# Advancing an attention pipeline by query block, both heads at once, instead of head by head

## The chip, the cores and the metric

The kernel runs on one core of one Trainium2 chip. The metric is device time in microseconds (us) of one execution. A core has five engines with queues of their own: TensorE (PE; its weight loads are listed as PEld), VectorE (DVE), ScalarE (ACT), GpSimd (POOL) and SyncE (SP), which issues the DMAs here. TensorE writes its results to PSUM, an accumulator memory; the other tiles lie in SBUF.

## What is computed

Two layers, each with one combined input projection, four groups of four attention heads (64 wide, sequence 1024, query blocks of 128 rows), a gate, an output projection and a layer norm:

```python
def hybrid_layer(x, ...):
    p = split_columns(einsum("bsd,de->bse", x, w_in))
    ...
    for i in range(S // Q_BLOCK):            # 8 query blocks of 128
        o_a = stick_breaking_block(a_q[:, q0:q1], a_k[:, :q1], a_v[:, :q1], qpos, kpos)
        o_b = diff_block(b_q[:, q0:q1], b_k[:, :q1], b_v[:, :q1], causal, bias_b, lam, lam_init, subln)
        o_c = dsa_block(...)                 # an indexer's top 256 keys, then softmax
        o_d = mla_block(...)
    y = concatenate(outs) * silu(p["gate"])
    y = einsum("bse,ed->bsd", y, w_out)
    return layer_norm(ALPHA * x + y, ln_g, ln_b)

def stick_breaking_block(q, k, v, qpos, kpos):
    z = einsum("bqhd,bkhd->bhqk", q, k) * HEAD_DIM ** -0.5
    log1m = where(strict, log_sigmoid(-z), 0.0)
    after = cumsum(log1m, axis=3, reverse=True) - log1m
    w = where(strict, exp(log_sigmoid(z) + after), 0.0)
    return einsum("bhqk,bkhd->bqhd", w, v)

def diff_block(...):                         # two softmax maps per head
    a = p[:, 0] - lam * p[:, 1]
    o = einsum("bhqk,bkhd->bqhd", a, v)
    return rms_norm(o, subln) * (1.0 - lam_init)
```

## The kernel before

The four groups are called a (stick-breaking), b (differential), c (sparse) and d (latent). Each has two units of two heads: a0, a1, d0, d1, b0, b1, c0, c1, in this order in a layer (`ORDER`, L42), after two units s0 and s1 that make the indexer's scores. Units walk over the eight query blocks; block i has n = 128 (i + 1) keys. A generator runs a unit and yields after each piece; between pieces the main loop (L1115) runs a stretch of background work (`Background`, `BGSEQ`): the input projections of later units, the gates, and from b1 on the output projection of the groups that are done (`g_out`). How much is a quota in us from `ORDER`, shared over a unit's steps by the weight (i + W0), W0 = 2. `with_topk` lays pieces of the top-k search (VectorE) between the steps of a0 and a1.

A unit (`softmax_pair`) has three stages per block. Stage 1 makes the scores of both heads in PSUM (`stick` for a, `on_rows` for the others) and turns them into weights in SBUF. In `stick` each head has a score buffer of its own, and per head five ScalarE instructions (absolute value, relu, exponential, logarithm, and the last exponential), a scan that runs backwards and a subtraction on VectorE. In `on_rows` VectorE scales and takes the minimum, ScalarE exponentiates; unit b has two maps per head, and from block 4 on two chunks of 512 keys. Stage 2 transposes a head's weights in blocks of 128 x 128 on TensorE into PSUM, from where ScalarE copies them to the tile PT (`transposed`); for b it first combines the two maps. Stage 3 multiplies PT and the values into one PSUM tile of four blocks (pv); after four blocks it multiplies the softmax sums out (rl) and `finalize` applies the gate and stores to y_d. For b `finalize` also makes the RMS norm: a square, a product with a matrix of 1/256 on TensorE (ms_b), a logarithm and an exponential.

`push` (L363) holds a queue of stages and advances by head: stage 1 of block i (with head 0), a stretch of projections, head 1's transposes of block i - 1; then for head 1 a second stretch, the values of block i - 1, head 0's transposes of block i.

PSUM has four tags: sc (two buffers of 1024 columns, the scores), mm (two of 512, the projections' sums, and in b and c the second transpose tile), tr (one of 512: transposes, rl, ms_b and others) and pv (one of 512). SBUF tiles of tag p (eight) hold weights, PT and results of the background; tag h (four halves) holds gates, outputs and the output projection's operands. The framework waits for data and buffers by itself, and its planner lays down the order on each engine before the program runs: code order is priority, and what it takes to be ready goes first. `Paced` passes matmuls through, so that their line is L92 or L95; no instruction is pinned by it here (`PIN_S` is 0).

Of the kernel before, what the change touches and what calls it, by code (L numbers as in the profile page):

```python
# [21 lines left out]
P = 128  # L22
# [21 lines left out]
TR_MM, PT_DVE = ('b0', 'b1', 'c0', 'c1'), ()  # L44
OUT_DVE = 1
PIN_A, PIN_S = 2, 0
OUT_AT = ('b1', 0.3)
FRAC, W0, W1 = 1, 2, 0.5
# [29 lines left out]


class Paced:  # L80


    def __init__(self, tc):
        self.tc, self.pin = tc, False

    def _issue(self, ins):
        if self.pin:
            self.tc.keep_in_program_order(ins)
        self.pin = False

    def matmul(self, *a, **k):
        self._issue(self.tc.nc.tensor.matmul(*a, **k))  # L92

    def transpose(self, *a, **k):
        self._issue(self.tc.nc.tensor.transpose(*a, **k))  # L95
# [3 lines left out]
def trunk(ctx: ExitStack, tc: tile.TileContext, t: dict, out: bass.AP, depth=DEPTH, dbg=None):  # L99
# [223 lines left out]
    def finalize(g, et, c, pv, gs, rl, subv):  # L323
        if g != 1:
# [3 lines left out]
        else:  # L328
            o = half("o_h")
            nc.scalar.activation(o, pv, AF.Copy)  # L330
            nc.vector.tensor_tensor(o, rl, o, op=ALU.mult)
            sq = half("sq_h")
            nc.scalar.activation(sq, o, AF.Square)
# [8 lines left out]
        nc.sync.dma_start(y_d[YPOS[et]][:, 512 * c:512 * c + 512], gs)  # L342

    def transposed(p, i, g, pair):
        nblk = i + 1
        pt = wrk([P, nblk, P], F32, "PT")
        for j0 in range(0, nblk, 4):
            m = min(4, nblk - j0)
            tr = mm_ps("trp") if j0 and f"{'abcd'[g]}{pair}" in TR_MM else tr_ps("trp")
            for j in range(m):  # L350
                te.transpose(tr[:, P * j:P * j + P], p[:, P * (j0 + j):P * (j0 + j) + P], ident)
            if j0 and f"{'abcd'[g]}{pair}" in PT_DVE:
                nc.vector.tensor_copy(pt[:, j0:j0 + m, :], tr[:, :P * m].rearrange("p (j n) -> p j n", j=m))
            else:
                with ahead(HP_T):
                    nc.scalar.activation(pt[:, j0:j0 + m, :], tr[:, :P * m].rearrange("p (j n) -> p j n", j=m), AF.Copy)  # L356
        return pt

    queue = []
    back = None  # L360
    te = Paced(tc)

    def push(w, pin, *stages):  # L363

        te.pin = pin & 1
        stages[0]()
        yield FRAC * w
        for it in list(queue):
            te.pin = pin & 2 if len(it) > 1 else pin & 4
            it.pop(0)()  # L370
            if not it:
                queue.remove(it)
        te.pin = False
        if len(stages) > 1:
            queue.append(list(stages[1:]))
        yield (1 - FRAC) * w

    def flush():
        while queue:
            for it in list(queue):  # L380
                it.pop(0)()
                if not it:
                    queue.remove(it)

    def softmax_pair(g, pair, scores, nmaps, nbt, scale, v, neglam=None, subv=None):
# [6 lines left out]
        def stick(i):  # L392

            n = P * (i + 1)
            z = {(h, 0): sc_ps("z") for h in range(2)}
# [3 lines left out]
            for h in range(2):  # L399
                zh = z[h, 0][:, :n]  # L400
                e, r = wrk([P, n], F32, "spe"), wrk([P, n], F32, "P0")

                nc.scalar.activation(e, zh, AF.Abs)
                nc.scalar.activation(r, zh, AF.Relu)
                nc.scalar.activation(e, e, AF.Exp, scale=-1.0)
                nc.scalar.activation(e, e, AF.Ln, bias=1.0)  # L406
                nc.vector.tensor_tensor_scan(backwards(r, n), backwards(r, n), backwards(e, n), 0.0, ALU.add, ALU.add)  # L407
                nc.vector.tensor_tensor(r, zh, r, op=ALU.subtract)
                nc.scalar.activation(r, r, AF.Exp)
                st[i]["res", h] = [r]  # L410

        def on_rows(i):

# [3 lines left out]
            p = {hm: wrk([P, n], F32, f"P{hm[1]}") for hm in maps}  # L417
            mx = {hm: small([P, 3], F32, "mx") for hm in maps}
            low = {hm: 3e38 for hm in maps}
            far = env["ns"].get(i) if g == 2 else None  # L420
            used = 0
            for o in range(0, n, 512):
# [5 lines left out]
                for lo, hi in ((o, min(o + w, near)), (a, o + w)):  # L428
                    if lo >= hi:
                        continue  # L430
                    for h, m in maps:
                        out = mx[h, m][:, used:used + 1]
# [7 lines left out]
                    used += 1  # L440
            for h, m in maps:
                nc.scalar.activation(p[h, m], p[h, m], AF.Exp, bias=low[h, m], scale=-1.0,  # L442
                                     accum_out=st[i]["ls"][:, m, h, i % 4:i % 4 + 1])
            for h in range(2):
                st[i]["res", h] = [p[h, m] for m in range(nmaps)]

        def stage1(i, h):
            i4 = i % 4
            if i4 == 0 and h == 0:
                st["ls"] = small([P, nmaps, 2, 4], F32, "ls", tag="ls", bufs=2)  # L450
            if h == 0:
                st[i] = dict(ls=st["ls"], pts=[])
            if h == 0:
                (on_rows if g else stick)(i)

        def stage2(i, h):
# [14 lines left out]
            d["pts"].append(transposed(p, i, g, pair))  # L471

        def stage3(i, h):
            if h == 0:
                return
# [6 lines left out]
            for j in range(i + 1):  # L482
                for hh in range(2):
                    te.matmul(pv[64 * hh:64 * hh + 64, P * i4:P * i4 + P], v[j // 4][:, j % 4, vo + 64 * hh:vo + 64 * hh + 64],
# [4 lines left out]
            elif i4 == 3:  # L489

                rl = tr_ps("rl")
                for k in range(4):
                    for hh in range(2):
                        te.matmul(rl[64 * hh:64 * hh + 64, P * k:P * k + P],
# [3 lines left out]
        for i in range(NB):  # L498
            for h in range(2):
                yield from push((i + W0) / (16 * W0 + 56), PIN_S, lambda: stage1(i, h), lambda i=i, h=h: stage2(i, h),  # L500
                                lambda i=i, h=h: stage3(i, h))
# [9 lines left out]
    for l in range(depth):  # L511
# [504 lines left out]
        def products(ps, maps, ops, i, o, w, rows_of, first=True, last=True):  # L1016

            qh, ql, kh, kl = ops
            for k, (x, y) in enumerate(((qh, kh), (ql, kh), (qh, kl))):
                for hm in maps:  # L1020
                    r = rows_of(*hm)
                    te.matmul(ps[hm][:, :w], x[r, P * i:P * i + P], y[r, o:o + w], start=first and k == 0,
                              stop=last and k == 2, tile_position=(r.start, 0))

        def score_a(pair):
            def f(ps, maps, i, o, w, near):
                tail = o + w == P * (i + 1)
                products(ps, maps, env[f"a{pair}t"], i, o, w, lambda h, m: slice(64 * h, 64 * h + 64), last=not tail)
                if tail:
                    for hm in maps:  # L1030
                        te.matmul(ps[hm][:, w - P:w], u_b, id_b, start=False, stop=True)
# [7 lines left out]
        def score_c(pair):  # L1039
            def f(ps, maps, i, o, w, near):  # L1040
# [3 lines left out]
                if msk:  # L1044
                    for hm in maps:
                        te.matmul(ps[hm][:, a - o:w], id_b, ns[i][:, a:o + w], start=False, stop=True)
            return f

        def score_d(pair):
            def f(ps, maps, i, o, w, near):  # L1050
# [3 lines left out]
                for k, (y, n) in enumerate(((krh, 64), (krl, 32))):  # L1054
                    for h, m in maps:
                        te.matmul(ps[h, m][:, :w], rq[64 * h:64 * h + n, P * i:P * i + P], y[64 * h:64 * h + n, o:o + w],
                                  start=False, stop=k == 1 and not tail, tile_position=(64 * h, 0))
                if tail:
                    for hm in maps:
                        te.matmul(ps[hm][:, w - P:w], id_b, v_b, start=False, stop=True)  # L1060
# [239 lines left out]
```

## Time and profile before

| | |
|---|---|
| median of 3 runs | 1829.26 us (1827.39 to 1833.37) |
| the profiled execution | 1826.64 us, span 1824.8 us |
| TensorE busy | 1680.8 us (92%), 10886 matmuls |
| VectorE busy | 1155.1 us (63%) |
| ScalarE busy | 860.9 us (47%) |
| GpSimd busy | 445.8 us (24%) |
[...]
| DMA | 205.70 MB, mean 113 GB/s |

Busy time counts an instruction from its start to its end; matmuls overlap, so the distance from one start to the next tells their cost better than their length. A timeline merges neighbouring instructions of a kind (x4); its first number is the first one's start. In brackets behind a row stands the engine's idle time before it, and what ended that.

### The profile page before, as it was taken

What the parts mean: (1) busy time and instruction counts of PE and PEld (TensorE: products, weight loads), DVE (VectorE), ACT (ScalarE), POOL (GpSimd) and SP (SyncE); (2) the same over time, 40 slices, a digit from 0 to 9 for tenths busy, and PEclk for the clock granted to TensorE, in tenths of its full rate; (3) what the DMA queues carried; (4) which work ended last, traced back from release to release, by engine and by line L of the source; (5) the groups of instructions that cost most, each with busy time, mean ns of one, the idle gap of its engine ahead of it and who ended that gap; (6) DMA issues with size and microseconds to landing.
All of it is one profiled execution on the core that took longest, in us unless ns stands there. A gap on an engine that the chain in (4) does not pass through costs nothing. (4 is left out here: it accounts for less than half of the span.)

```text
span 1824.8 us, 29123 instructions
## 1 busy us (share of the span) xinstructions
PE 1680.8 (92%) x10886; PEld 1246.0 (68%) x10886; DVE 1155.1 (63%) x2605; ACT 860.9 (47%) x1715; POOL 445.8 (24%) x406
## 2 busy tenths in 40 slices
PE   7998888899999999899999997989999999988997
PEld 5686666677676776576777765757776767765775
DVE  5777788865346445454866778898553555554448
ACT  3436757533355443345434466574334454433452
POOL 4232123422122312110322321233212222212012
PEclk9999979999999999899999998999999999998999
DMA  6221122525223236544331211235242322565343
GB/s 190 76 90 39 35 96 76 186 84 162 105 77 109 81 118 217 165 152 138 141 90 39 95 35 48 83 118 191 64 145 93 110 93 76 165 197 163 111 145 110
DMA packets 117034, 205.70 MB, mean 113 GB/s; under 512 B 11113, under 2 KB 41369, under 8 KB 116889
## 3 DMA queue, kind: packets, MB, share of 16 engines
q1 hardware_dynamic: 116888, 203.81, 33.9%
q8 instruction: 86, 1.41, 0.3%
q14 instruction: 60, 0.48, 0.1%
HBM read 131.92 MB, written 71.32 MB: 111 GB/s over the span
## 5 line engine op out<-in xcount | busy, mean ns | idle before, releaser
L236 PE MATMUL ps_pj<-xh,whi 128*128 128x512 f32 x832 | 349.2, 420 | 13.0 <-ACT xh L527 9.9
L197 POOL TENSOR_SCALAR whi<-wraw 128x512 fp32r<-128x512 f32 (+1 forms) x154 | 114.8, 746 | 923.1 <-PE ps_pj L236 573.8
L236 PE MATMUL ps_pj<-xl,whi 128*128 128x512 f32 x832 | 335.6, 403 | 0.4 <-DVE xl L528 0.4
L236 PE MATMUL ps_pj<-xh,wlo 128*128 128x512 f32 x832 | 334.7, 402 | 0.0
L356 ACT ACTIVATE PT<-trp 128x512 f32<-128x512 f32 (+3 forms) x384 | 182.0, 486 | 314.5 <-PE trp L95 307.6
L442 ACT ACTIVATE P<-P,mx 128x128 f32<-128x128 f32 (+7 forms) x256 | 195.9, 767 | 137.8 <-DVE mx L436 63.1
L95 PE MATMUL trp<-ident,P 128*128 128x128 f32 x1152 | 198.5, 287 | 32.9 <-ACT PT L356 12.0
L198 POOL TENSOR_TENSOR wlo<-wraw,whi 128x512 fp32r<-128x512 f32 (+1 forms) x154 | 216.0, 1403 | 14.0 <-PE ps_pj L236 1.4
L95 PEld LDWEIGHTS trp<-ident,P 128*128 128x128 f32 x1152 | 131.4, 142 | 101.1 <-ACT PT L356 33.4
L236 PEld LDWEIGHTS ps_pj<-xh,whi 128*128 128x128 f32 x832 | 160.2, 192 | 56.8 <-issue 23.1
L92 PE MATMUL pv<-PT,v 128*64 128x128 f32 x2304 | 190.1, 284 | 3.2 <-ACT PT L356 3.0
L236 PEld LDWEIGHTS ps_pj<-xh,wlo 128*128 128x128 f32 x832 | 159.6, 192 | 36.7 <-issue 2.6
L236 PEld LDWEIGHTS ps_pj<-xl,whi 128*128 128x128 f32 x832 | 160.7, 193 | 33.4 <-issue 5.2
L92 PEld LDWEIGHTS pv<-PT,v 128*64 128x64 f32 x2304 | 137.6, 138 | 60.0 <-issue 43.8
L438 DVE TENSOR_SCALAR_CACHE_REDUCE P<-ps_r 128x512 f32<-128x512 f32 (+3 forms) x160 | 83.4, 567 | 139.8 <-PE ps_r L92 120.2
L92 PE MATMUL ps_r<-op 64*128 64x512 f32 (+7 forms) x1152 | 156.5, 389 | 3.7 <-DVE P L438 3.0
L849 DVE SCALAR_TENSOR_TENSOR S<-rel,iw,S 128x512 f32<-128x512 f32 (+3 forms) x140 | 109.9, 787 | 36.4 <-ACT rel L843 30.6
L874 DVE TENSOR_SCALAR_CACHE_REDUCE junk<-S,t 128x1024 bf16<-128x1024 f32 (+1 forms) x132 | 124.2, 941 | 2.9
L407 DVE TENSOR_TENSOR_SCAN P<-P,spe 128x128 f32<-128x128 f32 (+7 forms) x64 | 91.8, 1435 | 43.3 <-ACT spe L406 43.3
L92 PEld LDWEIGHTS ps_r<-op 32*128 32x128 f32 (+1 forms) x1152 | 81.5, 184 | 55.1 <-issue 34.6
L258 PE MATMUL ps_v<-whi,xh 128*128 128x256 f32 x384 | 112.6, 294 | 0.3 <-DVE kl L296 0.3
L258 PE MATMUL ps_v<-wlo,xh 128*128 128x256 f32 x384 | 110.3, 288 | 0.0
(231 smaller groups left out, 2866.3 us busy)
## 6 DMA issues: line engine op xcount, KB each, us to landing
wraw<-in_wqk_dram SPq DMA_DIRECT2D x104, 256.0 KB, 2.6
g_d<-gate SPq DMA_DIRECT2D x32, 256.0 KB, 2.0
gs_h<-g_d SPq DMA_DIRECT2D x32, 256.0 KB, 3.7
y_d<-gs_h SPq DMA_DIRECT2D x32, 256.0 KB, 2.1
yraw<-y_d SPq DMA_DIRECT2D x32, 256.0 KB, 3.4
part_d<-xo SPq DMA_DIRECT2D x32, 256.0 KB, 2.7
tt<-part_d SPq DMA_DIRECT2D x16, 512.0 KB, 6.5
wraw<-in_wv_dram SPq DMA_DIRECT2D x24, 256.0 KB, 3.0
```

Source lines behind the costliest of these rows:

```text
L92: self._issue(self.tc.nc.tensor.matmul(*a, **k))
L95: self._issue(self.tc.nc.tensor.transpose(*a, **k))
L197: nc.gpsimd.tensor_scalar(hi, raw, 1.0, 0.0, op0=ALU.mult, op1=ALU.add)
L198: nc.gpsimd.tensor_tensor(lo, raw, fb(hi), op=ALU.subtract)
L236: nc.tensor.matmul(ps, a[:, k4, :], b[:, kb, 512 * c:512 * c + 512], start=(n == 0), stop=(n == 23))
L258: nc.tensor.matmul(pv, a[:, kb, P * sb:P * sb + P], b[:, k2, :], start=(n == 0), stop=(n == 23))
L356: nc.scalar.activation(pt[:, j0:j0 + m, :], tr[:, :P * m].rearrange("p (j n) -> p j n", j=m), AF.Copy)
L407: nc.vector.tensor_tensor_scan(backwards(r, n), backwards(r, n), backwards(e, n), 0.0, ALU.add, ALU.add)
L438: nc.vector.tensor_scalar(dst, src, -scale, low[h, m], op0=ALU.mult, op1=ALU.min, accum_out=out)
L442: nc.scalar.activation(p[h, m], p[h, m], AF.Exp, bias=low[h, m], scale=-1.0, accum_out=st[i]["ls"][:, m, h, i % 4:i % 4 + 1])
L849: nc.vector.scalar_tensor_tensor(s[:, o:o + w], r[:, h, :w], sc, s[:, o:o + w], op0=ALU.mult, op1=ALU.add)
L874: ins = nc.vector.tensor_scalar(junk[:, :P * (i + 1)], arr[i], th, None, op0=op, op1=ALU.add, accum_out=dst[:, k:k + 1])
```

## The change

`push` becomes `step`, which advances one query block with both heads: the scores of block i and both heads' transposes of block i - 1 (where there are two score chunks, b from block 4 on, the transposes alternate with them), one stretch of projections of twice the length, then the values of block i - 1. The normalisation product of b and what follows it is put off by one block. Transposes alternate between the buffers tr and mm in all units. In `stick` both heads share one score buffer for n up to 512, and ScalarE's five instructions and the subtraction do both at once. `Paced` goes, so that the matmuls of the pipeline carry their own lines.

```diff
-    def push(w, pin, *stages):
-        te.pin = pin & 1
-        stages[0]()
-        yield FRAC * w
-        for it in list(queue):
-            te.pin = pin & 2 if len(it) > 1 else pin & 4
-            it.pop(0)()
-            if not it:
-                queue.remove(it)
-        te.pin = False
-        if len(stages) > 1:
-            queue.append(list(stages[1:]))
-        yield (1 - FRAC) * w
+    pipe = dict(turn=[], values=[], late=[])
+
+    def step(w, scores, turn, values):
+        old = pipe["turn"], pipe["values"]
+        for k in range(max(len(scores), len(old[0]))):
+            for stage in (scores, old[0]):
+                if k < len(stage):
+                    stage[k]()
+        yield w
+        after(old[1])
+        pipe.update(turn=turn, values=values)
+
+    def after(values):
+        late, pipe["late"] = pipe["late"], []
+        for f in late + values:
+            f()
...
-            tr = mm_ps("trp") if j0 and f"{'abcd'[g]}{pair}" in TR_MM else tr_ps("trp")
+            tr = (mm_ps if k + j0 // 4 & 1 else tr_ps)("trp")
...
     def finalize(g, et, c, pv, gs, rl, subv):
...
+        def norm():
             ms = tr_ps("ms_b")
             for h in range(2):
                 r = slice(64 * h, 64 * h + 64)
-                te.matmul(ms[r], on256[r, :64], sq[r], start=True, stop=True)
+                nc.tensor.matmul(ms[r], on256[r, :64], sq[r], start=True, stop=True)
             nc.scalar.activation(sq, ms, AF.Ln, bias=eps_r, scale=4.0)
             nc.scalar.activation(sq, sq, AF.Exp, scale=-0.5)
             nc.vector.scalar_tensor_tensor(o, o, subv[:, 0:1], sq, op0=ALU.mult, op1=ALU.mult)
             nc.vector.tensor_tensor(gs, o, gs, op=ALU.mult)
+            out()
+
+        pipe["late"].append(norm)
...
         def stick(i):
             n = P * (i + 1)
-            z = {(h, 0): sc_ps("z") for h in range(2)}
+            if n <= 512:
+                zs = [sc_ps("z").rearrange("p (h n) -> p h n", h=2)[:, :, :n]]
+                z = {(h, 0): zs[0][:, h] for h in range(2)}
+            else:
+                zs = [sc_ps("z").unsqueeze(1)[:, :, :n] for _ in range(2)]
+                z = {(h, 0): zs[h][:, 0] for h in range(2)}
...
-            for h in range(2):
-                zh = z[h, 0][:, :n]
-                e, r = wrk([P, n], F32, "spe"), wrk([P, n], F32, "P0")
+            for k, zh in enumerate(zs):
+                nh = 2 // len(zs)
+                e, r = wrk([P, nh, n], F32, "spe"), wrk([P, nh, n], F32, "P0")
                 nc.scalar.activation(e, zh, AF.Abs)
                 nc.scalar.activation(r, zh, AF.Relu)
                 nc.scalar.activation(e, e, AF.Exp, scale=-1.0)
                 nc.scalar.activation(e, e, AF.Ln, bias=1.0)
-                nc.vector.tensor_tensor_scan(backwards(r, n), backwards(r, n), backwards(e, n), 0.0, ALU.add, ALU.add)
+                for h in range(nh):
+                    rb, eb = backwards(r[:, h], n), backwards(e[:, h], n)
+                    nc.vector.tensor_tensor_scan(rb, rb, eb, 0.0, ALU.add, ALU.add)
                 nc.vector.tensor_tensor(r, zh, r, op=ALU.subtract)
                 nc.scalar.activation(r, r, AF.Exp)
...
         for i in range(NB):
-            for h in range(2):
-                yield from push((i + W0) / (16 * W0 + 56), PIN_S, lambda: stage1(i, h), lambda i=i, h=h: stage2(i, h),
-                                lambda i=i, h=h: stage3(i, h))
+            yield from step((i + W0) / (8 * W0 + 28), stage1(i), [lambda i=i, h=h: stage2(i, h) for h in range(2)],
+                            [lambda i=i: stage3(i)])
```

`stage1` now returns a list: one function, or in b one for each chunk of 512 keys.

## Rows read from the trace of the kernel before

**Rows 1.** The page, first section: busy us, share of the span, instructions.

```profile
PE 1680.8 (92%) x10886; PEld 1246.0 (68%) x10886; DVE 1155.1 (63%) x2605; ACT 860.9 (47%) x1715; POOL 445.8 (24%) x406
```

**Rows 2.** The view of cores: span and mean granted clock.

```profile
core 0: 1824.8 us, clock 0.966
```

**Rows 3.** TensorE's waits: line, tile, what ended them; us in total, times, longest.

```profile
PE z L92 <- DVE P L408: 21.2, 18, 2.6
PE trp L95 <- ACT PT L356: 12.0, 18, 2.1
...
PE z L92 <- ACT rel L843: 8.0, 4, 3.1
...
PE ms_b L92 <- ACT sq_h L333: 6.4, 8, 1.5
PE ps_r L92 <- DMA krr<-kr_d: 5.7, 2, 3.2
...
PE trp L95 <- ACT sq_h L338: 3.3, 6, 0.8
...
PE trp L95 <- DVE hl L286: 0.4, 2, 0.2
```

**Rows 4.** Windows of a0 with a1, and c1: span, busy by engine, clock, DMA share.

```profile
141.00:368.00 227.00, 196.72 (x1089) 145.21 (x1089) 189.28 (x334) 145.04 (x265) 61.75 (x57) 0.92 0.26 86
...
827.00:866.00 39.00, 38.17 (x333) 26.23 (x330) 17.10 (x72) 23.25 (x54) 2.51 (x2) 1.00 0.38 127
```

**Rows 5.** Timeline of TensorE, a block of d0: start, us, instruction.

```profile
424.75 0.66 PE L95 MATMUL trp<-ident,P 128*128 128x128 f32 x4
425.34 0.73 PE L92 MATMUL ps_r<-op 64*128 64x512 f32 x4
...
431.61 0.39 PE L236 MATMUL ps_pj<-xh,wlo 128*128 128x512 f32 x1
431.84 0.60 PE L95 MATMUL trp<-ident,P 128*128 128x128 f32 x4
432.19 0.48 PE L236 MATMUL ps_pj<-xh,whi 128*128 128x512 f32 x1
```

**Rows 6.** Timeline of TensorE in c1: values between transposes and scores.

```profile
845.17 0.43 PE L92 MATMUL pv<-PT,v 128*64 128x128 f32 x2
845.53 0.50 PE L92 MATMUL ps_r<-op 64*128 64x512 f32 x2
```

**Rows 7.** Timeline of TensorE in a0 and a1: scores that wait for a buffer.

```profile
142.22 0.47 PE L92 MATMUL z<-kh,qh 64*128 64x128 f32 x1 [0.90 <-ACT rel L843]
...
160.40 0.50 PE L92 MATMUL z<-kh,qh 64*128 64x512 f32 x1 [0.76 <-DVE P L408]
...
239.17 0.44 PE L92 MATMUL z<-kh,qh 64*128 64x128 f32 x1 [2.36 <-DVE P L408]
```

**Rows 8.** Timeline of TensorE at c0's start: the normalisation product of b1's last blocks.

```profile
766.65 1.08 PE L92 MATMUL ms_b<-sq_h,on 64*64 64x512 f32 x4 [1.50 <-ACT sq_h L333]
768.57 0.33 PE L95 MATMUL trp<-ident,P 128*128 128x128 f32 x1 [0.85 <-ACT sq_h L338]
...
774.35 0.63 PE L806 MATMUL ps_o<-wlo,yhl 128*128 128x512 f32 x1
774.78 1.05 PE L806 MATMUL ps_o<-whi,yhl 128*128 128x512 f32 x2
```

**Rows 9.** A window behind that product; columns as in rows 4.

```profile
769.00:776.00 7.00, 6.60 (x18) 3.85 (x19) 3.68 (x14) 4.17 (x14) 0.00 (x0) 0.53 0.58 177
```

**Rows 10.** Groups by shape: busy us, mean ns of one, idle before; first three: 140 to 368 us.

```profile
L406 ACT ACTIVATE spe<-spe 128x1024 f32<-128x1024 f32 x4 | 4.3, 1072 | 0.0
L406 ACT ACTIVATE spe<-spe 128x512 f32<-128x512 f32 x4 | 2.5, 633 | 0.0
L407 DVE TENSOR_TENSOR_SCAN P<-P,spe 128x512 f32<-128x512 f32 x4 | 5.4, 1346 | 1.2 <-ACT spe L406 1.2
...
L356 ACT ACTIVATE PT<-trp 128x512 f32<-128x512 f32 x192 | 112.0, 592 | 177.4 <-PE trp L95 171.2 <-issue 2.9 <-DMA dq_d<-hl 2.6
```

More of the change, by code (lines that the diff above doesn't have):

```diff
@@ L77, in until @@
             self.budget -= self.step()
[L80 to L95, printed above, removed]
 @with_exitstack
@@ L348, in transposed @@
             m = min(4, nblk - j0)
-            tr = mm_ps("trp") if j0 and f"{'abcd'[g]}{pair}" in TR_MM else tr_ps("trp")
+            tr = (mm_ps if k + j0 // 4 & 1 else tr_ps)("trp")
             for j in range(m):
[L351 to L356, printed above, removed]
+                nc.tensor.transpose(tr[:, P * j:P * j + P], p[:, P * (j0 + j):P * (j0 + j) + P], ident)
+            with ahead(HP_T):
+                nc.scalar.activation(pt[:, j0:j0 + m, :], tr[:, :P * m].rearrange("p (j n) -> p j n", j=m), AF.Copy)
         return pt
-    queue = []
     back = None
-    te = Paced(tc)
-    def push(w, pin, *stages):
-        te.pin = pin & 1
-        stages[0]()
-        yield FRAC * w
-        for it in list(queue):
-            te.pin = pin & 2 if len(it) > 1 else pin & 4
-            it.pop(0)()
-            if not it:
-                queue.remove(it)
-        te.pin = False
-        if len(stages) > 1:
-            queue.append(list(stages[1:]))
-        yield (1 - FRAC) * w
-    def flush():
[L379 to L383, printed above, removed]
+    pipe = dict(turn=[], values=[], late=[])
[12 more added lines that the diff above has]
+            f()
+    def flush():
+        for f in pipe["turn"]:
+            f()
+        after(pipe["values"])
+        after([])
+        pipe.update(turn=[], values=[])
     def softmax_pair(g, pair, scores, nmaps, nbt, scale, v, neglam=None, subv=None):
@@ L439, in on_rows, with stage1 @@
                         low[h, m] = out
[L440 to L443, printed above, removed]
-            for h in range(2):
[L445 to L449, printed above, removed]
+                if o + w == n:
+                    for h, m in maps:
+                        nc.scalar.activation(p[h, m], p[h, m], AF.Exp, bias=low[h, m], scale=-1.0,
+                                             accum_out=st[i]["ls"][:, m, h, i % 4:i % 4 + 1])
+                    for h in range(2):
+                        st[i]["res", h] = [p[h, m] for m in range(nmaps)]
+            chunks = [lambda k=k, o=o: chunk(k, o) for k, o in enumerate(range(0, n, 512))]
+            return chunks if nmaps > 1 else [lambda: [f() for f in chunks]]
+        def stage1(i):
+            if i % 4 == 0:
                 st["ls"] = small([P, nmaps, 2, 4], F32, "ls", tag="ls", bufs=2)
[L451 to L454, printed above, removed]
+            st[i] = dict(ls=st["ls"], pts=[])
+            return on_rows(i) if g else [lambda: stick(i)]
         def stage2(i, h):
@@ L1021, in products @@
                     r = rows_of(*hm)
-                    te.matmul(ps[hm][:, :w], x[r, P * i:P * i + P], y[r, o:o + w], start=first and k == 0,
+                    nc.tensor.matmul(ps[hm][:, :w], x[r, P * i:P * i + P], y[r, o:o + w], start=first and k == 0,
                               stop=last and k == 2, tile_position=(r.start, 0))
```

59 lines of the change are left out of this document (28 added, 31 removed).

## The prediction

> **What bounds the kernel now.** I read the page first: TensorE is busy in 92% of the span [rows 1]. [...] Second I read the list of TensorE's waits [rows 3]: the long totals that belong to the attention pipeline are scores z waiting for VectorE's subtraction (21.2 us, 18 times), transposes waiting for ScalarE's copy of an earlier transpose (12.0 us, 18), z waiting for the indexer's relu (8.0), the normalisation product waiting for the square (6.4) and transposes waiting for the logarithm behind that product (3.3). Third the table by stage [rows 4]: in the stretch of the two stick-breaking units TensorE is busy 196.7 of 227 us at clock 0.92, and VectorE 189.3 of 227 us; there the two engines are close. In the last sparse unit TensorE is busy 38.2 of 39 us, so idle time is no reserve there, only hand-overs are. Last, timelines of single blocks [rows 5 to 8], which give the prices below.
>
> The order on TensorE isn't the order of the code: four transposes stand between two projection matmuls [rows 5], because the framework's planner fills a stall that it foresees with later work. So only stalls that it doesn't foresee and real extra work reach the time. That is why I take parts of the bounds, not all.
>
> **The change, part by part.** All blocks: 8 pairs x 8 query blocks x 2 layers = 128 steps, of which 16 are of unit b with two score chunks.
>
> *Hand-overs.* Scores and values use parts of the array (64 or 32 rows, 64 columns), projections and transposes the whole. Four transposes between values and scores hold TensorE 425.34 - 424.75 = 0.59 us, four in front of projections 432.19 - 431.84 = 0.35 us [rows 5]: two hand-overs cost 0.24 us more, 0.12 us each. Before, a block goes transposes (head 0), scores, projections, transposes (head 1), projections, values, transposes: whole-to-part or part-to-whole changes stand at T to scores, at the scores' end, at projections to values, at values to T. After: scores, T, T, projections, values, scores: one less, as values run straight into scores. Is that one dear? A pair of value matmuls that stands between transposes and scores takes 845.53 - 845.17 = 0.36 us [rows 6], of the size of the transposes' two changes, so I count it like the others. Gain 0.12 x 112 blocks = 13.4 us; in the 16 b blocks with two chunks the transposes of head 0 stand between the chunks, two changes more and one less: + 0.12 x 16 = 1.9. Sum **-11 us**; bounds 0 (the planner breaks the stretches up) and -0.12 x 128 = -15.
>
> *Two heads of unit a in one score buffer, for blocks 0 to 3.* Both score buffers (sc, two of them) were taken by the two heads of a block; now one holds both, so the next block's scores need no release. Of the waits these vanish: block 3's 0.76 us (at 160.40), the second buffer's 2.36 us at the start of a1 (239.17), and 0.90 us at the start of a0 (142.22) [rows 7]; 4.0 us a layer, **-8 us** in two. What is late next: the first buffer's own release at a unit's start stays, and blocks 4 to 7 keep two buffers and their waits. Bounds 0 and -(21.2 + 8.0) = -29.
>
> *The merged activations.* Five ScalarE instructions for 2n columns replace ten for n. One of them takes 0.633 us at 512 columns and 1.072 at 1024 [rows 10], so ScalarE's work falls, but head 0's scan now starts only after both heads. Until head 1's scan ends, the four instructions ahead of it and the scans (1.346 us each at 512 [rows 10]) took 8 x 0.633 + 1.346 = 6.4 us; now 4 x 1.072 + 2 x 1.346 = 7.0. The subtraction and the exponential behind are for both heads too, by the same pair of rows some 0.44 us longer each. So + 1.5 us at n = 512 and less below it; call it an estimate of 1 us over 4 blocks x 4 units = 16 us. Cover: block 3 of a0 is followed by 47.1 x 5/44 = 5.4 us of projections (the quota written in the code), the values of block 2 and the scores of block 4, some 8 us together (my estimate), where the whole chain takes 7.0 + 2 x 1.07 = 9.1. If that cover goes, all 16 us show. I take **+4**, bounds 0 and +16.
>
> *Transposes of both heads together, alternating between buffers tr and mm.* The single buffer tr made the second transpose wait for the copy: 12.0 us in 18 waits [rows 3]. With two buffers a copy of 0.59 us [rows 10] lies beside the next four transposes. I take **-5**, bounds 0 and -12. Against it: head 1's first transposes now always want an mm buffer, and mm's two buffers are those that projections accumulate in; after three of four pauses one is held by a half-done projection. If the other isn't drained, the transposes wait, and with them, as TensorE runs in order, the projections and values behind, and ScalarE's copies. The nearest row: in b and c the second transpose of four blocks of eight already uses mm, and waits for a projection's drain there sum to 0.4 us in 2 times [rows 3]. So near nothing per block; I take 0.05 x 128 = **+6**, bounds 0 and, at a full copy (0.59) plus the 0.1 of a hand-over each block, 0.7 x 128 = +90.
>
> *One stretch of projections, values at its end.* The same projections, in one piece: no instruction more, and SP issues the same DMAs. Operands of the next unit are fetched at the end of a step, of which there are half as many, so up to half a step later; the only wait for a load is the 5.7 us at d0's start [rows 3], where lateness could add its like: in the range, not in the sum. SP's and POOL's queues keep their order, only the normalised unit's y store follows one block later. In b, live tiles fall by one during the stretch. **0**.
>
> *Normalisation product one block later.* Before, behind the last values of four blocks, TensorE meets the product while VectorE and ScalarE still work on its operand: 1.50 us of idling, then 0.85 us until the logarithm frees tr [rows 8]; in total 6.4 us in 8 times and 3.3 us in 6 [rows 3]. A block later the square is long done, and the logarithm has values and scores to hide under. **-9.7 us**, bounds 0 and -9.7. The stretch behind one of these idlings runs at 0.53 of the clock for 7 us, one such in each layer [rows 9]; a matmul step there is 774.78 - 774.35 = 0.43 us [rows 8], against 0.23 us (431.84 - 431.61 [rows 5]). If the clock stays up, some 0.45 of two such stretches comes back, 6 us; I take **-4**, as transposes and copies idle there too. What it adds: three of the four half buffers stay held for a block, and the output products at c0's start use the same tag; the planner can bring the product forward, so 0.
>
> Sum: -11 - 8 + 4 - 5 + 6 - 9.7 - 4 = -27.7 us. Against the profiled execution, 1826.64 us (span 1824.8, 1.8 around it), 1798.9; the median of the runs lies 2.6 us above it, so **1801.5 us**.
>
> [...] In the last sparse unit 72 transposes with hardly a projection run at a granted clock of 1.00 [rows 4]. [...]
>
> **The rivals.** *Waits only move.* In the a stretch VectorE is busy 83% [rows 4]; a score buffer more lets TensorE run ahead only to wait for the same scan in the transposes. Without the -8 and the -5: -15, **1814**. For it: VectorE's share; against it: the planner has projections to put in.
>
> *Nothing arrives.* The planner's order comes out much as now, the gains of the hand-overs and waits below 5 us: **1827**. For it: transposes are spread among projections already.
>
> *Slower: the mm buffers.* Head 1's transposes meet a held and an undrained mm buffer at the start of every stretch. At 0.35 us for each of 128 blocks, half of the upper bound, + 45 in place of + 6: -27.7 + 39 = +11, **1840**. It decides from (27.7 + 6)/128 = 0.26 us per block on. Against it stand the 0.4 us of [rows 3]; for it, that units a and d, which never used mm for transposes, now do so in each block.
>
> *All of it.* Every bound: -15 - 29 - 12 - 9.7 - 6 = -72, **1757**. It needs VectorE to keep up.
>
> [...]
>
> **How the numbers follow.** Forecast 0.42, waits move 0.18, nothing 0.10, mm buffers 0.20, all 0.08, half clock 0.02. About 0.3% (5.5 us) is what a measurement here can tell from no change. Faster: 0.42 + 0.18 + 0.08 less 0.02 of edges = 0.66; same 0.12; slower 0.22. The forecast's own range is 1780 to 1818, from its smaller bounds; to hold 8 in 10 the range reaches down past it towards the full gain, 1768, and up over the mm case, 1845; what is left out is the half clock, most of the full gain and the worst of mm.
>
> **What the profile after would show.** Right: values run into scores; z's waits fall by some 8 us, all in blocks 0 to 3 and the units' starts; waits of the product and of the logarithm are gone; the clock by c0's start is 1.00. Wrong: transposes that wait for a projection's drain, or projections that wait for the transposes' copies (mm); transposes in a that wait for the exponential (chain longer than its cover); a longer wait for krr at d0 (fetch late). What would make the prediction wrong as a whole is a planner that lays the projections elsewhere: the page's rows would then differ in many groups by a little, with none of the above.

## The result, and the profile after

The changed kernel takes 2008.09 us (median; 1999.02 to 2014.46) where the kernel before takes 1828.33: ratio 1.0973, 95% interval 1.0923 to 1.1023. It is 180 us slower; a gain of 28 was forecast, and no rival stood near 2008.

First the page's busy line and the view of cores of after, beside [rows 1] and [rows 2]:

```profile
PE 1774.7 (88%) x10886; PEld 1317.4 (66%) x10886; DVE 1142.2 (57%) x2589; ACT 850.9 (42%) x1635; POOL 434.8 (22%) x406
core 0: 2009.3 us, clock 0.916
```

The number of matmuls is the same. TensorE's idle time rose from 1824.8 - 1680.8 = 144 us to 2009.3 - 1774.7 = 234.6, by 91 us, and its busy time by 94 for the same work. The mean granted clock fell with it, from 0.966 to 0.916. Stretches at 1.00 and at 0.50 are shown below; if all of the span lies at one of these two, my estimate is 0.034 x 2 x 1824.8 = 124 us at half clock before and 0.084 x 2 x 2009.3 = 338 now, and 214 us more at half speed lose 107 us of work, near the 94. So the loss is new idle time, and about as much again in busy time at a lower clock.

Where it lies, the windows tell, cut at each unit pair's first score matmul in layer 1, as a (a0 with a1), d, b, c (columns as in [rows 4]). Of the kernel before, and then of after:

```profile
141.00:368.00 227.00, 196.72 (x1089) 145.21 (x1089) 189.28 (x334) 145.04 (x265) 61.75 (x57) 0.92 0.26 86
368.00:521.00 153.00, 146.71 (x1105) 108.31 (x1103) 76.89 (x174) 61.25 (x136) 33.03 (x29) 0.99 0.33 109
521.00:733.00 212.00, 201.04 (x1389) 150.15 (x1385) 116.67 (x400) 94.28 (x215) 49.17 (x44) 1.00 0.38 126
733.00:865.00 132.00, 123.12 (x897) 85.97 (x895) 59.82 (x191) 61.11 (x141) 18.75 (x22) 0.96 0.46 151
```

```profile
140.00:399.00 259.00, 212.20 (x1120) 158.12 (x1122) 194.22 (x338) 143.28 (x229) 62.58 (x57) 0.86 0.26 83
399.00:542.00 143.00, 139.74 (x1034) 103.76 (x1029) 67.71 (x162) 54.73 (x129) 29.06 (x27) 0.99 0.30 100
542.00:820.00 278.00, 238.26 (x1417) 175.59 (x1416) 111.75 (x396) 95.58 (x215) 45.92 (x46) 0.88 0.29 98
820.00:959.00 139.00, 128.32 (x891) 90.08 (x891) 62.74 (x196) 63.17 (x144) 19.96 (x22) 0.92 0.45 146
```

Unit b lost 66 us a layer, a 32 and c 7; d gained 10. Layer 2 shows the same. The counts of matmuls must be read with the lengths: d is shorter mainly because 71 of its matmuls moved elsewhere, and a holds 31 more. In b 28 more matmuls explain little of 66 us; there the clock went from 1.00 to 0.88.

TensorE's waits in after, beside [rows 3]:

```profile
PE trp L338 <- ACT PT L340: 51.0, 18, 5.9
PE ps_r L1014 <- DVE cf L458: 28.8, 6, 7.5
PE z L1014 <- DVE P L400: 22.0, 11, 5.3
PE trp L338 <- DVE P L460: 16.8, 29, 1.2
PE ps_r L1014 <- DVE P L433: 15.9, 12, 2.5
...
PE ps_r L1014 <- DVE mx L431: 14.7, 18, 2.1
```

The normalisation product and its logarithm are gone from the list, as forecast. New are transposes that wait up to 5.9 us for a copy of an earlier transpose (2.1 before), and scores (`ps_r`) that wait for VectorE, up to 7.5 us.

**In a**, the timeline of after (ScalarE and TensorE, block 6 of a0):

```profile
211.94 1.26 PE L338 MATMUL trp<-ident,P 128*128 128x128 f32 x10
212.27 0.90 ACT L393 ACTIVATE spe<-z 128x896 f32<-128x896 f32 x1
...
217.13 0.96 ACT L395 ACTIVATE spe<-spe 128x896 f32<-128x896 f32 x1
217.97 0.61 ACT L340 ACTIVATE PT<-trp 128x512 f32<-128x512 f32 x1
...
218.64 0.69 PE L338 MATMUL trp<-ident,P 128*128 128x128 f32 x2 [5.44 <-ACT PT L340]
```

The scores of block 6 come first, so ScalarE takes up their activations: seven, from 212.27 to 217.97. The transposes of block 5 are issued right behind the scores and fill their three buffers; the first copy comes at 217.97, and TensorE, in order, idles 5.44 us with its projections behind it.

**In b**, the list of what ended VectorE's idle time before L433, the instruction that scales scores into a tile P of tag p (us, times; the whole run), and two of its rows in b1 of layer 1, then TensorE's next to them:

```profile
  PE ps_r L1052: 44.2, 16
  PE ps_r L1048: 39.7, 10
  PE pv L477: 38.3, 8
  PE ps_r L1014: 36.4, 14
  DMA cv_d<-v: 29.3, 4
  DMA g_d<-gate: 15.2, 6
  DMA b1k_d<-hl: 9.5, 4
```

```profile
727.06 0.42 DVE L433 TENSOR_SCALAR_CACHE_REDUCE P<-ps_r 128x256 f32<-128x256 f32 x1 [4.37 <-DMA cv_d<-v]
...
753.22 0.56 DVE L433 TENSOR_SCALAR_CACHE_REDUCE P<-ps_r 128x384 f32<-128x384 f32 x1 [10.29 <-DMA cv_d<-v]
```

```profile
728.45 0.79 PE L1014 MATMUL ps_r<-op 32*128 32x512 f32 x2 [4.61 <-DVE cf L458]
...
731.01 0.42 PE L238 MATMUL ps_v<-whi,xl 128*128 128x256 f32 x1
731.22 0.41 PE L238 MATMUL ps_v<-wlo,xh 128*128 128x256 f32 x1
...
734.30 0.28 PE L238 MATMUL ps_v<-wlo,xh 128*128 128x256 f32 x1
734.42 0.28 PE L238 MATMUL ps_v<-whi,xh 128*128 128x256 f32 x1
```

L433 reads scores and writes P. That a stored projection (`cv_d<-v`, `g_d<-gate`, `b1k_d<-hl`) or a value product (`pv`) ends its wait means that P had no slot: v, gate, hl and PT are tiles of tag p too. While VectorE stands there, the score buffer stays full and TensorE's next scores wait: the row names `cf`, VectorE's last instruction before them, but the cause is one row up, a landing DMA. The last four rows show the price behind a wait: the same matmuls start 0.21 us apart at 731, where the granted clock is 0.50 (window 728.4 to 734.0 us), and 0.12 us apart from 734.3 on, where it is 1.00 (734.2 to 739.0).

The slots can be counted in the code. In b a block has four P tiles (two heads, two maps). After puts the four of block i next to the four of block i - 1, not yet transposed: 8 of 8, nothing left for a projection's result or a PT whose values are still to come. Before, head 0 of i - 1 was transposed by then: 4 + 2 + one PT = 7. With transposes first it is 4 and two PT = 6. The count is an argument; the experiments test it.

### The profile page after: what moved, and what is told of

Same layout as the page of the kernel before. It is cut to its first block, busy times and chain, and to the rows that moved or that the text cites. A ratio compares the mean times of both kernels' runs of the same rounds, so it can differ in the third digit from the quotient of the medians.

```text
span 2009.3 us, 29019 instructions
## 1 busy us (share of the span) xinstructions
PE 1774.7 (88%) x10886; PEld 1317.4 (66%) x10886; DVE 1142.2 (57%) x2589; ACT 850.9 (42%) x1635; POOL 434.8 (22%) x406
## 5 line engine op out<-in xcount | busy, mean ns | idle before, releaser
L216 PE MATMUL ps_pj<-xh,whi 128*128 128x512 f32 x832 | 356.4, 428 | 15.2 <-ACT xh L519 9.0
L216 PE MATMUL ps_pj<-xh,wlo 128*128 128x512 f32 x832 | 340.7, 410 | 0.0
L177 POOL TENSOR_SCALAR whi<-wraw 128x512 fp32r<-128x512 f32 (+1 forms) x154 | 106.5, 692 | 1060.1 <-PE ps_pj L216 622.8
L340 ACT ACTIVATE PT<-trp 128x512 f32<-128x512 f32 (+3 forms) x384 | 174.9, 486 | 285.2 <-PE trp L338 257.6
L1014 PE MATMUL ps_r<-op 64*128 64x512 f32 (+7 forms) x1152 | 189.1, 418 | 61.2 <-DVE cf L458 28.8
L338 PEld LDWEIGHTS trp<-ident,P 128*128 128x128 f32 x1152 | 144.0, 157 | 127.3 <-ACT PT L340 73.6
L477 PE MATMUL pv<-PT,v 128*64 128x128 f32 x2304 | 202.5, 288 | 17.7 <-ACT PT L340 14.7
L216 PEld LDWEIGHTS ps_pj<-xh,whi 128*128 128x128 f32 x832 | 166.2, 200 | 69.9 <-issue 18.7
L433 DVE TENSOR_SCALAR_CACHE_REDUCE P<-ps_r 128x512 f32<-128x512 f32 (+3 forms) x160 | 86.1, 567 | 211.4 <-PE ps_r L1052 42.6
L1014 PEld LDWEIGHTS ps_r<-op 32*128 32x128 f32 (+1 forms) x1152 | 98.5, 201 | 121.6 <-issue 72.9
L238 PE MATMUL ps_v<-whi,xl 128*128 128x256 f32 x384 | 112.8, 294 | 0.0
```

The costliest lines, as they stand in the source:

```text
L177: nc.gpsimd.tensor_scalar(hi, raw, 1.0, 0.0, op0=ALU.mult, op1=ALU.add)
L216: nc.tensor.matmul(ps, a[:, k4, :], b[:, kb, 512 * c:512 * c + 512], start=(n == 0), stop=(n == 23))
L238: nc.tensor.matmul(pv, a[:, kb, P * sb:P * sb + P], b[:, k2, :], start=(n == 0), stop=(n == 23))
L338: nc.tensor.transpose(tr[:, P * j:P * j + P], p[:, P * (j0 + j):P * (j0 + j) + P], ident)
L433: nc.vector.tensor_scalar(dst, src, -scale, low[h, m], op0=ALU.mult, op1=ALU.min, accum_out=out)
L477: nc.tensor.matmul(pv[64 * hh:64 * hh + 64, P * i4:P * i4 + P], v[j // 4][:, j % 4, vo + 64 * hh:vo + 64 * hh + 64], pts[hh][:, j, :], sta ...
```

## The experiments

Below, A is the tiles of tag p in b, B ScalarE's copies in a behind the next block's activations, and C the alternation of score chunks and transposes in b. In the expectations of the first four runs theory A is both A and B, and rival B is something else: that the single long stretch of projections costs the time. That rival falls with the first run, which keeps the stretch. All runs differ from the changed kernel by the edit shown, unless it says otherwise; ratios are to the kernel before on the same chip.

**Transposes ahead of the scores, in all units.**

```diff
-        for k in range(max(len(scores), len(old[0]))):
-            for stage in (scores, old[0]):
-                if k < len(stage):
-                    stage[k]()
+        for f in old[0] + scores:
+            f()
```

> The changed kernel, but each step makes the transposes of block i - 1 before the scores of block i. Theory A (weights of both heads and both blocks are alive at once, so tag p's eight tiles run out in b, and in a the copies of the transposes queue behind the next block's activations): both go; the 67 us a layer in b and the 15 us a layer in a return, 2008 - 2 x 75 = about 1850 us or below. Rival B (the single long stretch of projections with the values behind it costs the time, whatever stands before it): no change, 2000 us or above. Rival C (the alternation of transposes and score chunks in b alone): about 2008 - 130 = 1880 us, with the copies' waits in a as they are.

1814.24 us, 0.9921 (0.9898 to 0.9944): the whole loss is gone, and a gain of 14 us stays. Its waits and its windows of a, d, b, c:

```profile
PE z L1012 <- DVE P L398: 19.6, 12, 1.9
PE trp L338 <- ACT P L399: 16.5, 11, 4.6
PE ps_r L1046 <- DMA krr<-kr_d: 14.9, 3, 6.9
...
PE trp L338 <- ACT PT L340: 6.2, 11, 0.9
```

```profile
141.00:377.00 236.00, 201.98 (x1128) 150.31 (x1128) 189.87 (x330) 142.93 (x229) 62.06 (x57) 0.92 0.26 84
377.00:530.00 153.00, 145.23 (x1061) 109.48 (x1062) 73.80 (x170) 58.50 (x131) 31.96 (x28) 0.94 0.33 106
530.00:744.00 214.00, 210.01 (x1445) 159.10 (x1444) 127.60 (x412) 98.34 (x223) 46.72 (x44) 0.99 0.41 136
744.00:861.00 117.00, 108.67 (x822) 74.16 (x823) 53.45 (x177) 57.04 (x131) 19.13 (x22) 1.00 0.47 152
```

So the loss comes from one thing, the transposes' place behind the scores. The waits for copies fell from 51.0 us to 6.2, and VectorE waits for no DMA ahead of its scaling any more. (a is 9 us longer than before with 39 matmuls more, c 15 shorter with 75 fewer: work that moved.) Two waits grew: the transposes' for a's last exponential, 16.5 us where the kernel before has 1.3, and that for the load at d0's start, 14.9 us for 5.7.

**The same in b alone, and in a alone.** An argument `first` of `step` chooses the order:

```diff
-        for k in range(max(len(scores), len(old[0]))):
+        if first:
+            for f in old[0] + scores:
+                f()
+        for k in range(0 if first else max(len(scores), len(old[0]))):
...
-                            [lambda i=i: stage3(i)])
+                            [lambda i=i: stage3(i)], first=g == 1)
```

> As the run before, but the transposes come first in unit b's steps alone; a, c and d keep scores first. Theory A: b's share returns, some 130 us, to about 1880 us, while transposes in a go on waiting for copies (about 50 us in all, longest near 6 us). Rival B: 2000 us or above. If VectorE's waits for values and for landed projections in b stay, tag p isn't what this order eases.

1866.73 us, 1.0205 (1.0187 to 1.0224): 141 us come back. TensorE's waits for copies stay: 52.0 us in 20 times.

With `first=g == 0`, a alone:

> The changed kernel with the transposes of the block before ahead of the scores in unit a alone. If the losses of a and of b are of separate origin and add up: a falls from 259 to about 236 us in each layer, b stays at 275 to 280, and the time is 2008 - 2 x 23 = 1962, between 1950 and 1975; TensorE's waits for ScalarE's copies in a go from 24.6 us a layer to under 6. If b's loss comes down from a (work that a left over), b falls too and the time comes under 1940.

1973.07 us, 1.0772 (1.0738 to 1.0806), 35 us less than after. Its windows of a and b:

```profile
141.00:379.00 238.00, 203.28 (x1124) 151.31 (x1124) 188.97 (x330) 143.74 (x230) 61.97 (x57) 0.91 0.26 83
...
529.00:803.00 274.00, 232.45 (x1409) 171.99 (x1410) 111.30 (x394) 94.80 (x213) 45.75 (x46) 0.90 0.30 100
```

a falls to its length with transposes first, b stays. The two losses have separate origins, and 141 + 35 = 176 of the 194 us between after and transposes-first lie in these two units.

**Scores first in d only** (`first=g != 3`), since d was shorter in after.

> Transposes before scores in a, b and c, scores first in d alone. In the runs so far d's two stretches were shorter with scores first (142.7 and 145.4 us in the changed kernel) than with transposes first (153.4 and 154.3 in e1_turn_first). Theory A (d has few live tiles and short chains, so there scores first is the better order): 1814 less some 20, 1795 us. Rival: d gained only because work had slipped into the late a before it, and the gain doesn't add: 1814 us.

1819.81 us, 0.995 (0.9927 to 0.9972): no gain over transposes-first everywhere. So d had not become better in after, it had less to do.

**A, by adding slots.** Nine tiles of tag p, paid with one buffer of the tile nb:

```diff
-N_B, N_P, N_H, N_W, N_R, N_S = 17, 8, 4, 4, 2, 10
+N_B, N_P, N_H, N_W, N_R, N_S = 17, 9, 4, 4, 2, 10
...
-        tl = sp.tile([P, 2, 256], F32, tag="nb", bufs=2, name="nb")
+        tl = sp.tile([P, 2, 256], F32, tag="nb", bufs=1, name="nb")
```

> The changed kernel with nine tiles of tag p in place of eight; the bias tile of b and c has one buffer in place of two to make room, which can only cost. Theory A: a good part of b's 134 us returns, at least 60, 1950 us or below, and VectorE's waits for landed projections (cv_d, g_d, b1k_d, c0q_d) shrink by half or more. Rivals B and C: no tile is short, so 2008 us or a little above.

1943.64 us, 1.0651 (1.0609 to 1.0692), 64 us less than after. What ends VectorE's idle time before L433 now, whole list, and the window of b:

```profile
  PE ps_r L1014: 68.0, 15
  PE ps_r L1052: 44.1, 16
  PE ps_r L1048: 40.0, 10
  DMA b1k_d<-hl: 4.8, 2
```

```profile
538.00:792.00 254.00, 231.44 (x1451) 172.68 (x1452) 113.53 (x402) 96.57 (x221) 48.02 (x46) 0.92 0.33 109
```

Waits for `pv`, `v` and `gate` are gone by one tile, and b is 24 us a layer shorter. Most of b's loss isn't slots, though: 40 us a layer stay against transposes-first. Eleven tiles (`N_B, N_P = 15, 11`, nb as here):

> The changed kernel with eleven tiles of tag p (eight before; room from two tiles of tag b, of which 15 are left, and one bias buffer). Theory A: with nine tiles b fell from 278 to 254 us a layer; with eleven no VectorE wait for a landed projection or for values is left in b, and b comes near 214 us: 2008 - 2 x 64 = 1880 us, a's 259 us unchanged or a little less. Rival C (the alternation of chunks and transposes in b): b stays near 250 us, 1945 us.

1967.19 us, 1.0737 (1.0693 to 1.0782): no more gain, 24 us worse than nine, where 1880 was expected. No DMA is left in that list, yet b stays at 255 us; a grew to 270. Two tiles of tag b had paid for it, so I took these alone (`N_B, N_P = 15, 8`, one nb):

> The changed kernel with eight tiles of tag p as it has, but 15 tiles of tag b (17 in it) and one buffer for the tile nb (two), which is what eleven p tiles were paid with. If these cost the 24 us by which eleven p tiles were slower than nine (paid with nb alone): 2008 + 24 = 2032, between 2020 and 2045, with a longer by 7 to 12 us a layer. If the eleven tiles themselves cost it (another order): 2000 to 2016.

2025.48 us, 1.1071 (1.1036 to 1.1107), 17 us above after, with a at 269 us. Within the noise, some 11 us on each of these differences, the missing b tiles account for the 24 us.

**A, by taking a slot from the kernel before** (`N_P` from 8 to 7, nothing else).

```diff
-N_B, N_P, N_H, N_W, N_R, N_S = 17, 8, 4, 4, 2, 10
+N_B, N_P, N_H, N_W, N_R, N_S = 17, 7, 4, 4, 2, 10
```

> The kernel before with seven tiles of tag p instead of eight. Theory A: before the change a block's first head is transposed ahead of the next block's scores, so seven weight tiles live at once in b where the change has eight and more; one tile less brings the old order to the same edge, and b grows by 20 to 40 us a layer, 1870 to 1910 us. Rival: the old order has slack, below 1840 us.

1874.46 us, 1.0237 (1.0194 to 1.028): 43 us slower. What ends VectorE's idle time before the same instruction, there L438, and the window of b:

```profile
  PE ps_r L92: 111.8, 44
  DMA cv_d<-v: 23.9, 4
...
  DMA b1k_d<-hl: 4.8, 2
```

```profile
535.00:753.00 218.00, 201.78 (x1373) 150.95 (x1372) 113.48 (x396) 93.80 (x213) 48.22 (x44) 0.98 0.37 122
```

With eight tiles the same list of the kernel before has no DMA:

```profile
  PE ps_r L92: 122.2, 48
  ACT PT L356: 17.6, 2
...
```

The old order shows after's waits as soon as its one spare tile is gone. Their price in b is small there, though: 218 us a layer where before has 212, not the 20 to 40 us more that were expected; 11 us a layer more lie in a (238 against 227). So this run shows that the old order needs its eight tiles, not what a full tag costs b. Transposes first with ten tiles (`N_B, N_P = 16, 10`, one nb) is the counterpart:

> e1_turn_first with ten tiles of tag p (sixteen of tag b, one bias buffer). Theory A: with transposes first the tiles are no longer short, so more of them bring little: 1800 to 1814 us. If the time falls by 20 us or more, tag p is still a limit there.

1826.54 us, 0.9987 (0.996 to 1.0014): no faster than with eight, some 12 us slower with a b tile and an nb buffer fewer. That order wants no more tiles.

**B, by moving the copies.** First their priority for the planner:

```diff
-HP_W, HP_S, HP_T, HP_A, HP_B = 0, 20, 0, 0, 0
+HP_W, HP_S, HP_T, HP_A, HP_B = 0, 20, 60, 0, 0
```

> The changed kernel with one number changed: the planner takes the copy of a transpose 60 instructions earlier than its place, ahead of the next block's activations on ScalarE. Theory A, its second half: the transposes' waits for copies in a fall from 51 us to some 10, and 20 to 35 us return, about 1980 us; b stays slow. Rival B: nothing, 2008 us. If the waits go and the time doesn't follow, they were cover for something else (VectorE in a).

1991.86 us, 1.088 (1.0842 to 1.0917); the waits fell only to 44.0 us in 19 times. In the timeline six activations in place of seven still stand ahead of the first copy in block 6, so this told little on B. Then another engine, in unit a alone:

```diff
+    pt_by = [False]
...
+                if pt_by[0]:
+                    nc.vector.tensor_copy(pt[:, j0:j0 + m, :], tr[:, :P * m].rearrange("p (j n) -> p j n", j=m))
+                else:
...
+            pt_by[0] = g == 0
```

> The changed kernel, but in unit a VectorE, not ScalarE, copies the transposed weights out of PSUM. Theory B (in a, the copies stand on ScalarE behind six or seven activations of the next block): TensorE's waits for the copies in a, 24.6 us in 8 times in one layer, fall under 8 us, since VectorE's longest single piece there, a scan, takes 2.0 us; a shortens from 259 us to 238 to 250 and the whole to 1965 to 1995. Rival (it is the place of the transposes behind the scores that costs, whoever copies): the waits keep 15 us or more in a layer, under the name of VectorE's copy, as VectorE holds scans, subtractions and the indexer's search there; a stays at 255 or more and the time at 2000 to 2025.

2032.43 us, 1.1104 (1.107 to 1.1138); the first of TensorE's waits in a of layer 1 is now

```profile
PE trp L340 <- DVE PT L343: 22.1, 8, 6.4
```

against 24.6 us in 8 times for ScalarE's copies in after. The waits are the rival's (15 us or more), though the time is above its range too (and VectorE's longest scan in a of after takes 2.4 us, 1024 wide, where 2.0 was named); B falls in its narrow form: it isn't ScalarE's queue alone. In block 6 VectorE is in the indexer's search when the transposes are issued, and a scan stands between its first two copies. That any engine which copies is by then at work on the new block is my reading; the run shows it for these two.

**C: no alternation.** All score chunks, then all transposes:

```diff
-        for k in range(max(len(scores), len(old[0]))):
-            for stage in (scores, old[0]):
-                if k < len(stage):
-                    stage[k]()
+        for f in scores + old[0]:
+            f()
```

> The changed kernel, but all score chunks of a block come before the transposes of the one before; in b the transposes no longer stand between the chunks. Rival C: b returns, 1880 us. Theory A: the eight weight tiles of two blocks are alive just as long or longer, so nothing is gained, 2000 us or above.

2007.03 us, 1.0975 (1.0917 to 1.1032): no difference. C falls.

**The change's other parts, one undone at a time, with transposes first.** Beside 0.9921 of that kernel:

Each head its own score buffer and activations in a:

```diff
-            if n <= 512:
-                zs = [sc_ps("z").rearrange("p (h n) -> p h n", h=2)[:, :, :n]]
...
+            z = {(h, 0): sc_ps("z") for h in range(2)}
...
-            for k, zh in enumerate(zs):
-                nh = 2 // len(zs)
+            for h in range(2):
+                zh = z[h, 0][:, :n]
```

> e1_turn_first with a's stick-breaking as it was: a score buffer and five activations for each head at every size. The prediction gave -8 us to the shared buffer and +4 to the longer chain, so undoing both should cost 4 us: 1818. Rival: a's stretches grew from 227 to 236 us a layer in e1_turn_first through the merged chain (transposes wait 16.5 us for a's last exponential there), so undoing it saves 10 to 18 us: 1796 to 1804.

1828.14 us, 0.9987 (0.9956 to 1.0018): above both expectations.

The normalisation product at once:

```diff
-        pipe["late"].append(norm)
+        norm()
```

> e1_turn_first with unit b's normalisation product behind its values at once, as before the change. The prediction gave the delay -9.7 us of waits and -4 of clock: 1814 + 14 = 1828, with the product's waits for the square back at 6 us. Rival: the planner hid most of it anyway, 1814 to 1818.

1825.0 us, 0.9982 (0.996 to 1.0005). The product's waits for the square come back as 1.4 us, not 6; those for its logarithm are 3.4 us in 6 times.

The second transpose buffer only where before had it:

```diff
-            tr = (mm_ps if k + j0 // 4 & 1 else tr_ps)("trp")
+            tr = (mm_ps if j0 and bc else tr_ps)("trp")
...
-            d["pts"].append(transposed(p, i + 1, h))
+            d["pts"].append(transposed(p, i + 1, h, g in (1, 2)))
```

> e1_turn_first with the transposes' buffers as before the change (tr alone, and mm for the second tile in b and c). The prediction gave the alternation -5 us for the waits on copies and +6 for contention in mm: 1813 to 1815. Rival: with both heads' transposes in one run, one buffer makes each wait for the last copy, 12 to 25 us more, 1826 to 1839, and the transposes' waits for copies rise above 12 us.

1854.97 us, 1.014 (1.0096 to 1.0184): slower than even the rival said, and not by its road. Transposes wait 7.6 us for copies, against 6.2 with transposes first and both buffers. TensorE's idle time is the same, 136 us; its busy time is 1716.1 us against 1677.8, at a clock of 0.963 against 0.962.

## Why the prediction was wrong

**The step that failed** is "One stretch of projections, values at its end", with its sentence "In b, live tiles fall by one during the stretch. **0**". I counted tiles in the stretch and not at the moment before it, where the new order holds two blocks' P tiles at once, 8 of 8. Priced at nothing, it holds about a third of a loss of 180 us: one more tile gives 64 us back, 48 of them in b (278 to 254 us a layer).

**A second omission** lies in the same place, and it is the larger. I priced the order scores, transposes only as hand-overs and as buffers tr and mm. What the scores set going on the other engines, ahead of the copies that transposes need, had no term. It costs a some 22 us a layer (259 against 236 to 238), and in b it is what nine and eleven tiles leave, some 40 us a layer (254 and 255 us against 214 with transposes first). What exactly the rest of b waits for isn't settled: with nine tiles b's idle time comes in many short waits for VectorE, of the combined weights (7.9 us in 15 times) and of the scaling; with transposes first they are gone but for 0.5 us in 2 times, and no run took these alone. The cover that I named for other terms, projections, could not help: they stand behind the waiting transposes on TensorE.

**Hand-overs**, -11: no run measured their price. Counted in the traces, in order of start, the changes between whole-array and part-array matmuls fell from 836 to 712 in after, 124 fewer where I had 96; with transposes first they rose to 914. So the count came as forecast, the gain, if it came, was inside a loss of 180, and the 14 us of transposes first owe it nothing. **Shared score buffer and merged activations**, -8 + 4 = -4: undone with transposes first, they are worth 0.0066 of 1828, 12 us, within some 7 either way. The wait that I feared, of the transposes for the exponential, is there (16.5 us in 11 times, 9.8 in 6 with the heads apart), but the sum is a gain, larger than I took. It isn't the gain I foresaw: the waits of scores z for VectorE and the indexer's relu are 25.9 us with the shared buffer and 27.2 without, not 8 apart. That the sign is right is in part luck. **Two buffers for the transposes**, -5 and +6: worth 0.0219 x 1828 = 40 us, some 9 either way, my largest mis-sizing of a part that works. I had taken the gain from the waits of the old order, but the waits for copies hardly move (6.2 and 7.6 us); the 40 us are busy time of TensorE. With one buffer the transposes stand in 350 runs in the trace, with two in 256, so the planner seems to lay other work between them; what that costs and why isn't shown. The rival of the mm buffers, forecast at 1840, didn't show: no transpose waits for a projection's drain in the lists of after and of transposes first, projections wait for transposes' copies 2.4 us in 6 times in after, and doing without those buffers costs time. **Normalisation a block later**, -9.7 - 4 = -13.7: the waits of [rows 3] left as foreseen, and undoing it costs 0.0061 x 1828 = 11 us, some 6 either way. Undone one at a time, then, these three parts are worth 12, 40 and 11 us, and yet the whole kernel with transposes first gains only 14. If the parts add up, which no run tests, the rest of the change costs around 50 us even in that order. That would be the advance by block itself, for which I had only a gain, in the hand-overs; the longer wait for the load at d0 is 9 us of it.

**Transposes at half clock**, 0.02 in the chances: no run shows the term. In the c1 stretch of [rows 4], where 72 transposes are 11.4 of TensorE's 38.2 busy us, the granted clock is 1.00, and with transposes first the b stretch holds the same transposes as after's, among other matmuls, at 0.99. None of these stretches is transposes alone, though. Where the clock is 0.50 in after, from 728.4 to 734.0 us, it follows a wait of 4.61 us:

```profile
722.00:728.00 6.00, 1.84 (x15) 1.23 (x13) 1.63 (x9) 2.01 (x6) 0.00 (x0) 0.94 0.24 91
728.40:734.00 5.60, 5.34 (x24) 4.78 (x25) 2.21 (x8) 2.09 (x6) 0.00 (x0) 0.50 0.22 79
```

**What would show it wrong.** The list had the mm drain, the exponential and the load at d0. None of them carried the loss; the load's wait left the list of after. With transposes first, where the loss is gone, two of these signs came: 16.5 us of waits for the exponential, and 14.9 us for the load at d0's start against 5.7, a term I had kept out of the sum. A line "VectorE waiting for a DMA before it scales scores" would have been the right one; [rows 3] couldn't show it, since VectorE never waits for a DMA there in the kernel before, with its one spare tile. The missing view was a count of slots by the code, at each point of the new order.

## What to carry to other kernels

When a change lets two blocks of a pipeline be alive at once, count the buffers of every shared tag at the fullest moment, with everything else that draws on the tag; here one tile more in a tag that had become exactly full was worth 64 us of 2008. Where an engine keeps to its order, as TensorE did here in the 5.44 us with its projections behind waiting transposes, put first what finishes old work and frees buffers, and then what starts new work: the same change with its transposes ahead of the scores is 0.8% faster than the kernel before, instead of 9.7% slower. And don't price a new wait on TensorE by its length alone: here 91 us of new idle time came with 94 us more of busy time, at a mean granted clock of 0.916 in place of 0.966.

## What the runs showed of the hardware

Here a wait cost more than its length. In b of after 29 us a layer of new idle time came with a clock of 0.88 in place of 1.00 and 37 us more of busy time. Behind a single wait of 4.61 us the engine ran 5.6 us at 0.50, its matmuls 0.21 us apart, not 0.12 as from 734.3 us on, at 1.00. And the row that names VectorE's `cf` as what ended six waits, 28.8 us, means a DMA each time: in all six an L433 whose wait a DMA had ended (`cv_d` four times, `b1k_d` twice) started 1.2 to 1.4 us before the score matmul. The chain has to be followed one engine further.
